# Three more column-pair groups of each up projection as 1024-column blocks with a seven-product pair, in a decoder trunk on one core

## The chip, the cores and the metric

The kernel runs on one core of a Trainium2 chip. The metric is the device time of one launch in microseconds, from the first instruction to the last of that core. The kernel before takes 2167.38 us as the median of three runs (2167.01 to 2168.72). A profile of one execution of it gives the rows quoted below.

## The reference

The input is x, 256 positions of 2048 features in float32. It passes one layer of gated linear attention, one layer of block attention (with 256 positions there is one block of keys, so it is plain causal attention with a position bias), and after each of them a gated ConvFFN. Each starts with an RMS norm and adds its result to x.

```
def conv_ffn(x, norm_w, w_up, conv_w, conv_b, w_down):
    S = x.shape[1]
    h = rms_norm(x, norm_w) @ w_up                 # 2048 -> 11264
    hp = jnp.pad(h, ((0, 0), (CONV_WIDTH - 1, 0), (0, 0)))
    acc = conv_b
    for j in range(CONV_WIDTH):
        acc = acc + conv_w[j] * hp[:, j:j + S]
    a, u = jnp.split(acc, 2, axis=-1)
    return (jax.nn.silu(a) * u) @ w_down           # 5632 -> 2048

h = h + gla_mixer(...)      # q, k, v, g = rms_norm(h) @ w_in; gated; @ w_out
h = h + conv_ffn(h, ...)
k, v = rms_norm(h) @ w_kv;  h = h + moba_mixer(h, ..., k, v)
h = h + conv_ffn(h, ...)
```

The two up projections (2048 x 11264) and the two down projections (5632 x 2048) are most of the work.

## The kernel before

**Matrix products.** TensorE works on operands that were split in two parts of reduced width: `whi` is the weight rounded by a cast on ScalarE (L151), `wlo` the rest, by a subtraction on VectorE (L153). The activations are kept the same way (`xw`: high half, then low half). A product is high x high + low x high + high x low, so three matmuls of 512 columns each. Two forms exist. `gemm_tok` (lines L305 and L308 in the profile) makes 512 output columns at a time: a step is one weight piece of 1024 columns (two rows of 128 features by 512 columns), 12 matmuls. `down` (L361) makes 1024 output columns and all 256 positions as a 2 x 2 grid of products per *pair* of 256 input features. A plain pair takes eight products in two steps of 12 matmuls, 24 in all. A pair marked + in `ORDERS` takes seven products (Strassen's scheme): 21 matmuls. For it VectorE makes sums of the weight (`t13`, `t24`: L112 to L114) that are split like weights, and sums of the activations: `whole` adds the high and low part of one pair (L328), `combine` makes four 128-wide parts from it (`comb`, L318 to L321), and splits them by a cast (L437, ScalarE) and a subtraction (L438, VectorE). At the end of a block VectorE adds the product sums up (`c`, L416 to L430).

**The weight stream.** Weights come by SP's queue in pieces of 128 x 2048 (`wraw`), and `WeightStream.prefetch` splits them a few steps ahead of TensorE, in rings of three buffers and more. `latest` holds the last pair of split instructions; what is issued under `behind()` is ordered after these two on its engine. Each engine runs its instructions in the order of its list, and that list is set by a scheduler before the launch, which can hoist instructions that depend on nothing late.

**Up projection.** Layer by layer, 22 column groups J of 512 columns (256 of the a half, 256 of the u half) run through `gemm_tok`. `square` scales the result (ScalarE) and transposes it (VectorE) into `z`; one step later POOL's queue stores it (`turned`), two steps later four POOL loads bring it back with features on the partitions (`upT`), and from step 7 `convolve` runs (ScalarE: `au`, then VectorE). `after(n, ...)` counts these steps of TensorE.

**Around it.** The gla gates (`gate`, `gated`) use the same way through memory, from step 12 for heads 2 and 3; their result `go` feeds the output projection. The k block, the g block and the mq block (1024 columns of k, g and the queries) use `down` with results that stay on chip (`DIRECT`). dn0 and dn1 are the down projections, with combinations that `convolve` makes early for pairs 1 to 13 (`EARLY`); pairs 15 and 17 go through `combine_parts`. At the start ACT's queue loads the norm weights `gn` and the first two pieces of x (`h`), while SP's queue loads the first weights in three cuts.

Of the kernel before, what the change touches and what calls it, by code (L numbers as in the profile page):

```python
# [37 lines left out]
def _order(text):  # L38

    words = text.replace("|", " ").split()  # L40
    return [(int(k.rstrip("+")), k.endswith("+")) for k in words], len(text.split("|")[1].split())
# [9 lines left out]
            _order("0 1+ 2 3+ 4 5+ 6 7+ 8 9+ 10 11+ 12 13+ 14 15+ 16 17+ 18+ | 19 20 21")],  # L51
    "k": [_order("0 1+ 2 3+ 4+ | 5 6 7")],
    "mq": [_order("0 1 2+ 3 4 | 5 6 7")],
    "g": [_order("0 2 5 1+ 3+ 4+ | 6 7")],
}
DIRECT = ("k", "mq", "g")


TURNS = ((0, (1, 2)), (0, (1, 2)), (1, (0, 1)), (1, (0, 1)), (1, (1, 2)), (1, (1, 2)))
# [108 lines left out]

@with_exitstack
def trunk(ctx: ExitStack, tc: tile.TileContext, xT, x_tok, cst, msk, w1p, w2a, w_k, w_qa, w_v2, w_v, w_gs, w_g, w_go,  # L170
          w_up0, w_dn0, w_kk, w_kv, w_mq, w_mqs, w_mo, w_up1, w_dn1, rel, onehot, out):
    nc = tc.nc
    V, A, T = nc.vector, nc.scalar, nc.tensor

# [1 line left out]
    big = ctx.enter_context(tc.tile_pool(name="big", bufs=38))  # L176
    raw = ctx.enter_context(tc.tile_pool(name="raw", bufs=3))
    parts = ctx.enter_context(tc.tile_pool(name="parts", bufs=3))
    tmp = ctx.enter_context(tc.tile_pool(name="tmp", bufs=6))
    small = ctx.enter_context(tc.tile_pool(name="small", bufs=2))  # L180
    banks = ctx.enter_context(tc.tile_pool(name="banks", bufs=8, space=PSUM))
    dram = ctx.enter_context(tc.tile_pool(name="dram", bufs=1, space=DRAM))
# [10 lines left out]
    def accs():  # L193
# [1 line left out]

    ws = WeightStream(tc, raw, parts)
    plan = [(w_v2, 1, 16384), (w_v, 2, 8192), (w_k, "k", None), (w_qa, 2, 8192), (w_gs, "g", None), (w_g, 2, 8192), (w_go, "go", None),
            (w_up0, FT // 2, 8192), (w_dn0, "dn0", None),
            (w_mq, (0,), 8192), (w_mqs, "mq", None), (w_mq, (1,), 8192), (w_kk, 4, 8192), (w_kv, 4, 8192), (w_mo, "mo", None),
            (w_up1, FT // 2, 8192), (w_dn1, "dn1", None)]  # L200
    for w, groups, cols in plan:
        if cols is None:
            for g, order in enumerate(ORDERS[groups]):
                ws.add_quads(w, g, order, groups in ("go", "mo"), groups == "mo")
            continue
        for g in range(groups) if isinstance(groups, int) else groups:
            ws.add(w, g, cols)
# [16 lines left out]
    V.memset(mhalf, -0.5)  # L224
    gn = keep.tile([128, KT], F32, name="gn")

    def load_x(p, queue=nc.sync):
        for i in range(2) if p == 0 else (slice(0, 2),):
            queue.dma_start(h[p][:, i], xT[p].rearrange("a (b c) -> a b c", b=2)[:, i])

    load_x(0, A)
    A.dma_start(gn, cst[:, C_GN:C_GN + KT])
    A.preload_act_table_set("natural_log_exp_and_others")
    load_x(1, A)

    ws.cuts = {0: ((0, 512), (512, 1024), (1024, 2048)), 1: ((0, 1024), (1024, 2048))}
    ws.lead[2, 0] = [lambda: nc.sync.dma_start(cs[:, :C_CW], cst[:, :C_CW])]
    for p, at in ((2, (1, 1024)), (3, (2, 0)), (4, (3, 0)), (5, (4, 0)), (6, (5, 0)), (7, (6, 0))):
        ws.lead.setdefault(at, []).append(lambda p=p: load_x(p))
# [44 lines left out]
    def after(steps, job):  # L284
        later.append((cur[0] + steps, job))
# [10 lines left out]
    def gemm_tok(xs, groups=1, evacuate=lambda ps: ps):  # L296
        out_ = [accs() for _ in range(groups)]
        for q0 in range(0, KT, 2):
            for ps in out_:
                hi, lo = step()  # L300
                for ks in ((0,), (1,)) if cur[0] < 3 and groups > 1 else ((0, 1),):
                    tiles_ = [(q0 + k, t, k * 512) for k in ks for t in range(2)]
                    for x0 in (0, S):
                        for kt, t, c in tiles_:
                            T.matmul(ps[t], xs(kt)[:, x0 + 128 * t:x0 + 128 * t + 128], hi[:, c:c + 512],  # L305
                                     start=kt == 0 and x0 == 0, stop=False)
                    for kt, t, c in tiles_:
                        T.matmul(ps[t], xs(kt)[:, 128 * t:128 * t + 128], lo[:, c:c + 512],  # L308
                                 start=False, stop=kt == KT - 1)
        got = out_ if groups > 1 else evacuate(out_[0])  # L310
        ws.prefetch(cur[0])
        return got
# [13 lines left out]
    def combine_parts(k, xs, into):  # L326
        t = temp("whole")
        V.tensor_add(t, xs[k][:, :, :S], xs[k][:, :, S:])  # L328
        combine(k, [(t[:, i, :128], t[:, i, 128:]) for i in range(2)], into)

    def sevens(name):
        return {k for order, _ in ORDERS[name] for k, seven in order if seven}

    def down(name, xs, combos, res, done, jobs):

        for b, (order, n_tail) in enumerate(ORDERS[name]):
            loaded = (name, b) != ("dn1", 1)
            new = [k for k, seven in order if seven and k not in combos]
            todo = {i: list(js) for i, js in jobs.get(b, {}).items()}
            for k in new:  # L340
                at = next(i for i, (k_, _) in enumerate(order) if k_ == k)
                todo.setdefault(max(at - 2, 0), []).append(lambda k=k: combine_parts(k, xs, combos))
            p = {}
            left = dict.fromkeys(range(1, 9), 0)
            for k, seven in order:
# [429 lines left out]
    down("g", nrm.xs, x_sums, None, gate_rows, {})  # L775
    for hd in (2, 3):
        z = gemm_tok(xs, 1, lambda ps: gate(hd, ps))
        through(hd, z, [(12 + i, lambda f, c=2 * hd + i: gated(c, f)) for i in range(2)])

    def ffn(layer, nrm, then):  # L780
        xs = rows(nrm.xs)
        hid, sums = [], {}
        whole = [None, None]
        cw = C_CW + layer * 3 * 2 * FT
        cb = C_CB + layer * 2 * FT
        turned = dram.tile([FT // 2, 16, 32, 4, 64], F32, name=f"turned{layer}")
# [12 lines left out]

        def load(J):  # L800
            f = slot([128, 4, S], F32, "upT")
            for q in range(4):
                nc.gpsimd.dma_start(f[32 * q:32 * q + 32].rearrange("p a (i c) -> p (a i) c", i=4),  # L803
                                  turned[J][:, :, q, :].rearrange("a r c -> r a c"))
            return f

        def convolve(j, t):
            au = temp("au")
            with ws.behind():
                for i in range(2):  # L810
                    n = i * FT + j
                    A.activation(au[:, i, :], t[:, i, :], AF.Identity, bias=col(cb + n),  # L812
                                 scale=col(cw + 2 * 2 * FT + n))
            for i in range(2):
                n = i * FT + j
                V.scalar_tensor_tensor(au[:, i, 1:], t[:, i, :S - 1], col(cw + 2 * FT + n), au[:, i, 1:],  # L816
                                       op0=OP.mult, op1=OP.add)
                V.scalar_tensor_tensor(au[:, i, 2:], t[:, i, :S - 2], col(cw + n), au[:, i, 2:],  # L818
                                       op0=OP.mult, op1=OP.add)
            A.activation(au[:, 0, :], au[:, 0, :], AF.Silu)  # L820
            V.tensor_mul(au[:, 0, :], au[:, 0, :], au[:, 1, :])
            if j % 2 == 0:
                hid.append(slot([128, 2, 2 * S], F32R, "hid"))
            split(hid[-1][:, j % 2, :S], hid[-1][:, j % 2, S:], au[:, 0, :])
            whole[j % 2] = (au[:, 0, :128], au[:, 0, 128:])
            if j % 2 and j // 2 in EARLY:
                combine(j // 2, whole, sums)

        f = {}
        for J in range(FT // 2):  # L830
            z = gemm_tok(xs, 1, square)
            after(1, lambda J=J, z=z: store(J, z))
            after(2, lambda J=J: f.update({J: load(J)}))
            for i in range(2):
                after(7 + 2 * i, lambda J=J, i=i: convolve(2 * J + i, f[J][:, 2 * i:2 * i + 2, :]))
        then(hid, sums)

    def scratch(name):
# [276 lines left out]

def _pairs(w):
    k, n = w.shape
    return _groups(w.reshape(k, 2, n // 256, 128).transpose(0, 2, 1, 3).reshape(k, n), 512)


def _buckets():
# [66 lines left out]
```

## Time and profile before

| | |
|---|---|
| time of the profiled execution | 2167.28 us |
| its span | 2165.5 us |
| start of the up projection of layer 0 | 375.56 us |
| start of dn0 | 855.2 us |
| mq block | 1108.6 us on |
| start of the up projection of layer 1 | 1454.54 us |
| start of dn1 | 1934 us |
| loads of `upT` | 176, 4.9 us from issue to landing (median) |

A page of the profile gives busy time by engine, the chain of work that ended last, and groups of instructions (line, engine, operation, count, busy time and mean length, idle time before them and what ended it). PE is TensorE's matmul row, PEld its weight loads, DVE is VectorE, ACT ScalarE, POOL GpSimd, SP the sync engine. Matmuls are pipelined: the length shown for one (0.39 us) is not the spacing between two starts. In a timeline, each row has the start, the length from the first start to the last end, and in brackets the idle time before it and what ended it.

### The profile page before, as it was taken

The numbers are of one execution on the slowest core, as the hardware profiler recorded it, in microseconds if no ns is written. First come the engines' busy times: TensorE is split into PE (matmuls) and PEld (weight loads), VectorE is DVE, ScalarE is ACT, GpSimd is POOL, SyncE is SP. The second block draws the span as 40 slices with busy tenths as digits, with TensorE's granted clock in tenths as the row PEclk, the third lists the DMA queues.
The fourth block names the chain that finished last, engine by engine and source line by source line (L and its number), as shares of the span: only waits on it lengthen the run. The fifth ranks groups of instructions, "written<-read, shape, count | busy, mean of one in ns | idle before, by whom it ended". The sixth has DMA issues, their size and how long they took to land.

```text
span 2165.5 us, 27041 instructions
## 1 busy us (share of the span) xinstructions
PE 2158.0 (100%) x9666; PEld 1789.5 (83%) x9666; DVE 1671.6 (77%) x2317; ACT 1301.1 (60%) x1881; POOL 291.5 (13%) x448
## 2 busy tenths in 40 slices
PE   9999999999999999999999999999999999999999
PEld 7888888888888888888888888888888888888887
DVE  6787788677777767898977787775777777779987
ACT  7656665565655656555566676565656565655554
POOL 1011111111111111000022241011111111110000
PEclk9999999999999999999999999999999999999999
DMA  8465676677777777675676887566787777775655
GB/s 321 178 232 196 214 263 241 219 234 251 236 247 237 247 237 244 212 253 211 234 262 246 269 270 240 213 234 225 236 248 235 249 235 248 237 252 214 233 199 171
DMA packets 90313, 510.10 MB, mean 236 GB/s; under 512 B 13714, under 2 KB 14754, under 8 KB 40259
## 3 DMA queue, kind: packets, MB, share of 16 engines
q1 hardware_dynamic: 60290, 417.05, 55.5%
q0 software_dynamic: 29024, 90.28, 14.6%
q8 instruction: 75, 1.23, 0.2%
q10 hardware_dynamic: 864, 1.06, 0.1%
q14 instruction: 60, 0.48, 0.1%
HBM read 463.22 MB, written 45.11 MB: 235 GB/s over the span
## 4 chain that ended last, share of the span: by engine, by line
PE 99%; DMA 1%; DVE 0%; ACT 0%; issue 0%; ACTq 0%; DVEq 0%
PE acc L305 42%; PE p L361 34%; PE acc L308 21%; PE hf L859 0%; DMA wraw<-w_go 0%; PE sT L705 0%; PE o L722 0%; PE s L972 0%; DMA h<-xT 0%; PE z L562 0%; PE o L508 0%; PE s L970 0%; DVE wlo L153 0%; PE o L507 0%; PE o L506 0%; PE o L505 0%
## 5 line engine op out<-in xcount | busy, mean ns | idle before, releaser
L153 DVE TENSOR_TENSOR wlo<-wraw,whi 128x1024 fp32r<-128x1024 f32 (+1 forms) x786 | 924.1, 1186 | 379.8 <-ACT whi L151 363.6
L151 ACT CAST whi<-wraw 128x1024 fp32r<-128x1024 f32 (+1 forms) x786 | 794.9, 1021 | 630.0 <-PE acc L305 390.6
L305 PE MATMUL acc<-whi,xw 128*128 128x512 f32 x3456 | 856.5, 390 | 1.3 <-ACT xw L268 1.3
L305 PEld LDWEIGHTS acc<-whi,xw 128*128 128x128 f32 x3456 | 648.9, 188 | 136.9 <-ACT xw L268 2.0
L308 PE MATMUL acc<-wlo,xw 128*128 128x512 f32 x1728 | 463.6, 390 | 0.0
L308 PEld LDWEIGHTS acc<-wlo,xw 128*128 128x128 f32 x1728 | 324.7, 188 | 67.4
L361 PE MATMUL p<-whi,hid 128*128 128x512 f32 x1058 | 284.4, 389 | 0.0
L361 PEld LDWEIGHTS p<-whi,hid 128*128 128x128 f32 x1058 | 198.4, 188 | 41.1
L151 ACT CAST whi<-t 128x1024 fp32r<-128x1024 f32 x100 | 102.9, 1052 | 84.6 <-PE p L361 70.4
L361 PE MATMUL p<-wlo,hid 128*128 128x512 f32 x529 | 153.1, 389 | 0.0
L803 POOL DMA_DIRECT2D upT<-turned x176 | 114.1, 655 | 147.1 <-DMA turned<-z 58.2
L153 DVE TENSOR_TENSOR wlo<-t,whi 128x1024 fp32r<-128x1024 f32 x100 | 119.9, 1221 | 15.0 <-PE p L361 8.1
L361 PE MATMUL p<-whi,comb 128*128 128x512 f32 x400 | 129.8, 389 | 0.0
L305 PE MATMUL acc<-whi,xkv 128*128 128x512 f32 x512 | 127.9, 391 | 0.0
L797 POOL DMA_DIRECT2D turned<-z x44 | 34.1, 775 | 679.1 <-DVE au L816 572.9
L361 PEld LDWEIGHTS p<-wlo,hid 128*128 128x128 f32 x529 | 99.3, 188 | 20.6
L305 PEld LDWEIGHTS acc<-whi,xkv 128*128 128x128 f32 x512 | 94.6, 188 | 18.7
L812 ACT ACTIVATE au<-upT,cs 128x256 f32<-128x256 f32 x176 | 95.8, 593 | 17.3 <-DMA upT<-turned 17.3
L361 PEld LDWEIGHTS p<-whi,comb 128*128 128x128 f32 x400 | 75.0, 188 | 15.5
L361 PE MATMUL p<-whi,xw 128*128 128x512 f32 x314 | 82.9, 389 | 0.0
L816 DVE SCALAR_TENSOR_TENSOR au<-upT,cs,au 128x255 f32<-128x255 f32 x176 | 77.0, 472 | 6.3 <-ACT au L812 6.1
L818 DVE SCALAR_TENSOR_TENSOR au<-upT,cs,au 128x254 f32<-128x254 f32 x176 | 80.5, 478 | 0.0
(241 smaller groups left out, 1897.5 us busy)
## 6 DMA issues: line engine op xcount, KB each, us to landing
wraw<-w_up SPq DMA_DIRECT2D x176, 1024.0 KB, 5.2
wraw<-w_dn SPq DMA_DIRECT2D x88, 1024.0 KB, 5.0
turned<-z POOLq DMA_DIRECT2D x44, 512.0 KB, 3.5
upT<-turned POOLq DMA_DIRECT2D x176, 128.0 KB, 4.9
wraw<-w_go SPq DMA_DIRECT2D x16, 1024.0 KB, 5.9
wraw<-w_kk SPq DMA_DIRECT2D x16, 1024.0 KB, 5.9
wraw<-w_kv SPq DMA_DIRECT2D x16, 1024.0 KB, 5.9
wraw<-w_mo SPq DMA_DIRECT2D x16, 1024.0 KB, 4.9
```

What stands on the lines that cost most here:

```text
L151: one = nc.scalar.copy(hi[:, a:b], src[:, a:b])
L153: two = nc.vector.tensor_sub(lo[:, a:b], src[:, a:b], hi[:, a:b].bitcast(F32))
L305: T.matmul(ps[t], xs(kt)[:, x0 + 128 * t:x0 + 128 * t + 128], hi[:, c:c + 512], start=kt == 0 and x0 == 0, stop=False)
L308: T.matmul(ps[t], xs(kt)[:, 128 * t:128 * t + 128], lo[:, c:c + 512], start=False, stop=kt == KT - 1)
L361: T.matmul(p[n], x[xi], w[wi][:, 512 * f:512 * f + 512], start=n not in begun, stop=left[n] == 0)
L797: nc.gpsimd.dma_start(turned[J].rearrange("(a i) r q c -> (i r) a (q c)", a=4), z.rearrange("p (a q) t c -> p a (q t c)", a=4))
L803: nc.gpsimd.dma_start(f[32 * q:32 * q + 32].rearrange("p a (i c) -> p (a i) c", i=4), turned[J][:, :, q, :].rearrange("a r c -> r a c"))
L812: A.activation(au[:, i, :], t[:, i, :], AF.Identity, bias=col(cb + n), scale=col(cw + 2 * 2 * FT + n))
L816: V.scalar_tensor_tensor(au[:, i, 1:], t[:, i, :S - 1], col(cw + 2 * FT + n), au[:, i, 1:], op0=OP.mult, op1=OP.add)
L818: V.scalar_tensor_tensor(au[:, i, 2:], t[:, i, :S - 2], col(cw + n), au[:, i, 2:], op0=OP.mult, op1=OP.add)
```

## The change

Four things are changed in the kernel. First, in each layer's up projection the groups J = 0, 4, 8 and 12 are each joined with the next one to a block of 1024 columns through `down("up", ..., only=b)`. Block 0 has two seven-product pairs, blocks 1 to 3 one. The other 14 groups stay in `gemm_tok`. The convolution starts at step 9, but for the last two groups. Second, `combine_parts` is issued under `behind()` in every `down`. Third, the gates' products of heads 2 and 3 start at steps 10 and 11, and the order of the first loads is set. Fourth, `temp` buffers go from 6 to 7, and the scratch of the software DMA from 4096 to 2048 bytes.

```diff
+    "up": [_order("0 1 2 3+ 4 5+ | 6 7")] + [_order("0 1 2 3+ 4 | 5 6 7")] * 3,
-DIRECT = ("k", "mq", "g")
+DIRECT = ("k", "mq", "g", "up")
+BLOCKS = (0, 4, 8, 12)
+GROUPS = [j for j in range(FT // 2) if j not in BLOCKS and j - 1 not in BLOCKS]
...
-    tmp = ctx.enter_context(tc.tile_pool(name="tmp", bufs=6))
+    tmp = ctx.enter_context(tc.tile_pool(name="tmp", bufs=7))
...
-    def load_x(p, queue=nc.sync):
-        for i in range(2) if p == 0 else (slice(0, 2),):
-            queue.dma_start(h[p][:, i], xT[p].rearrange("a (b c) -> a b c", b=2)[:, i])
-
-    load_x(0, A)
-    A.dma_start(gn, cst[:, C_GN:C_GN + KT])
-    A.preload_act_table_set("natural_log_exp_and_others")
-    load_x(1, A)
+    def load_x(p, i=slice(0, 2), queue=nc.sync):
+        return queue.dma_start(h[p][:, i], xT[p].rearrange("a (b c) -> a b c", b=2)[:, i])
+
+    begun = load_x(0, 0, A)
+    with tc.issue_after(begun.ins):
+        begun = A.dma_start(gn, cst[:, C_GN:C_GN + KT])
+    with tc.issue_after(begun.ins):
+        A.preload_act_table_set("natural_log_exp_and_others")
+        load_x(1, queue=A)
...
+    ws.lead[0, 0] = [lambda: load_x(0, 1)]
...
+    def combine_late(k, xs, into):
+        with ws.behind():
+            combine_parts(k, xs, into)
+
-    def down(name, xs, combos, res, done, jobs):
+    def down(name, xs, combos, res, done, jobs, only=None):
 
         for b, (order, n_tail) in enumerate(ORDERS[name]):
+            if only not in (None, b):
+                continue
...
-                todo.setdefault(max(at - 2, 0), []).append(lambda k=k: combine_parts(k, xs, combos))
+                todo.setdefault(max(at - 2, 0), []).append(lambda k=k: combine_late(k, xs, combos))
...
-        through(hd, z, [(12 + i, lambda f, c=2 * hd + i: gated(c, f)) for i in range(2)])
+        through(hd, z, [(8 + hd + i, lambda f, c=2 * hd + i: gated(c, f)) for i in range(2)])
...
-        f = {}
+        f, first = {}, {}
+
+        def onto(J, z):
+            after(1, lambda: store(J, z))
+            after(2, lambda: f.update({J: load(J)}))
+            for i in range(2):
+                after((9 if J < FT // 2 - 2 else 7) + 2 * i, lambda i=i: convolve(2 * J + i, f[J][:, 2 * i:2 * i + 2, :]))
+
+        def up_rows(t, J, x):
+            if t == 0:
+                first[J] = slot([128, 16, 2, 32], F32, "z")
+            A.activation(x, x, AF.Copy, scale=nrm.woven[:, t:t + 1])
+            V.transpose(first[J][:, :, t, :], x.rearrange("p (a b) -> p a b", b=32))
+            if t:
+                onto(J, first[J])
+
+        x_sums = {}
         for J in range(FT // 2):
-            z = gemm_tok(xs, 1, square)
-            after(1, lambda J=J, z=z: store(J, z))
-            after(2, lambda J=J: f.update({J: load(J)}))
-            for i in range(2):
-                after(7 + 2 * i, lambda J=J, i=i: convolve(2 * J + i, f[J][:, 2 * i:2 * i + 2, :]))
+            if J in BLOCKS:
+                b = BLOCKS.index(J)
+                down("up", nrm.xs, x_sums, None, lambda t, c, x: up_rows(t, J + c - 2 * b, x), {}, b)
+            elif J in GROUPS:
+                onto(J, gemm_tok(xs, 1, square))
...
-    nc = bacc.Bacc("TRN2", target_bir_lowering=False, num_devices=1, dynamic_dma_scratch_size=4096)
+    nc = bacc.Bacc("TRN2", target_bir_lowering=False, num_devices=1, dynamic_dma_scratch_size=2048)
```

The rest of the diff lays the weights out for it (`w_up0s`, `w_up1s` for the blocks, `w_up0`, `w_up1` for the groups that stay) and adds them to the plan of the stream.

What `behind()` does to the order shows in the k block. VectorE's rows there, from before the high part whi_1008 of the second seven-product pair is subtracted; `comb_1000` and `comb_1005` are the combination of the third pair, `t24_959` is the last weight sum of the second pair, `t13_1026` the first of the third. Before:

```order
L153 TENSOR_TENSOR wlo_974<-wraw_830,whi_973 128x1024
L112 TENSOR_TENSOR t13_1026<-wraw_891 128x1024
L438 TENSOR_TENSOR comb_1005<-comb_1000,comb_1005 128x4x128
L114 TENSOR_TENSOR t24_959<-wraw_857,t24_959 128x512
L153 TENSOR_TENSOR wlo_988<-wraw_857,whi_987 128x512
L153 TENSOR_TENSOR wlo_1009<-wraw_857,whi_1008 128x1024
L113 TENSOR_TENSOR t24_1027<-t13_1026,wraw_891 128x512
L153 TENSOR_TENSOR wlo_1032<-t13_958,whi_1031 128x1024
L153 TENSOR_TENSOR wlo_1048<-t24_959,whi_1047 128x1024
```

And now:

```order
L156 TENSOR_TENSOR wlo_988<-wraw_857,whi_987 128x512
L341 TENSOR_TENSOR whole_998<-xw_275 128x512
L117 TENSOR_TENSOR t24_959<-wraw_857,t24_959 128x512
L156 TENSOR_TENSOR wlo_1009<-wraw_857,whi_1008 128x1024
L156 TENSOR_TENSOR wlo_1032<-t13_958,whi_1031 128x1024
L331 TENSOR_TENSOR comb_1000<-whole_998 128x128
L333 TENSOR_TENSOR comb_1000<-whole_998 128x128
L332 TENSOR_TENSOR comb_1000<-comb_1000,whole_998 128x128
L334 TENSOR_TENSOR comb_1000<-whole_998,comb_1000 128x128
L115 TENSOR_TENSOR t13_1026<-wraw_891 128x1024
L457 TENSOR_TENSOR comb_1005<-comb_1000,comb_1005 128x4x128
L156 TENSOR_TENSOR wlo_1048<-t24_959,whi_1047 128x1024
```

The whole and the four parts of the third pair, which stood some fifty rows ahead, now stand among the weights of the second. ScalarE's rows at the same place, before:

```order
L437 CAST comb_1005<-comb_1000 128x4x128
L151 CAST whi_987<-wraw_857 128x512
L151 CAST whi_1008<-wraw_857 128x1024
L151 CAST whi_1031<-t13_958 128x1024
L151 CAST whi_1047<-t24_959 128x1024
L151 CAST whi_1054<-wraw_891 128x512
```

And now:

```order
L154 CAST whi_987<-wraw_857 128x512
L154 CAST whi_1008<-wraw_857 128x1024
L154 CAST whi_1031<-t13_958 128x1024
L456 CAST comb_1005<-comb_1000 128x4x128
L154 CAST whi_1047<-t24_959 128x1024
L154 CAST whi_1054<-wraw_891 128x512
```

The cast of the combination passed from ahead of the second pair's weights to a place in front of their last, whi_1047.

In the mq block (seven-product pair 2) VectorE has, before, with `whole_9251` and `comb_9253` of that pair:

```order
L328 TENSOR_TENSOR whole_9251<-xw_8189 128x512
L153 TENSOR_TENSOR wlo_9174<-wraw_9059,whi_9173 128x1024
L318 TENSOR_TENSOR comb_9253<-whole_9251 128x128
L320 TENSOR_TENSOR comb_9253<-whole_9251 128x128
L153 TENSOR_TENSOR wlo_9190<-wraw_9059,whi_9189 128x1024
L319 TENSOR_TENSOR comb_9253<-comb_9253,whole_9251 128x128
L153 TENSOR_TENSOR wlo_9213<-wraw_9124,whi_9212 128x1024
L112 TENSOR_TENSOR t13_9207<-wraw_9171 128x1024
L321 TENSOR_TENSOR comb_9253<-whole_9251,comb_9253 128x128
```

And now, behind the queries' scaling and transposes that follow the block of columns before (the same tiles have the numbers 9373 and 9375):

```order
L981 TENSOR_TENSOR q_9350<-q_9350,rr_9359 128x1024
L537 STREAM_TRANSPOSE z_9362<-q_9350 128x4x4x32 x2
L156 TENSOR_TENSOR wlo_9366<-wraw_9246,whi_9365 128x1024
L341 TENSOR_TENSOR whole_9373<-xw_8311 128x512
L156 TENSOR_TENSOR wlo_9401<-wraw_9293,whi_9400 128x512
L156 TENSOR_TENSOR wlo_9422<-wraw_9293,whi_9421 128x1024
L331 TENSOR_TENSOR comb_9375<-whole_9373 128x128
L333 TENSOR_TENSOR comb_9375<-whole_9373 128x128
L156 TENSOR_TENSOR wlo_9440<-t13_9329,whi_9439 128x1024
L332 TENSOR_TENSOR comb_9375<-comb_9375,whole_9373 128x128
L334 TENSOR_TENSOR comb_9375<-whole_9373,comb_9375 128x128
L457 TENSOR_TENSOR comb_9380<-comb_9375,comb_9380 128x4x128
```

The combination passed behind the queries' reduction, scaling and transposes and between the low parts of its own pair.

More of the change, by code (lines that the diff above doesn't have):

```diff
@@ L170, in trunk @@
 def trunk(ctx: ExitStack, tc: tile.TileContext, xT, x_tok, cst, msk, w1p, w2a, w_k, w_qa, w_v2, w_v, w_gs, w_g, w_go,
-          w_up0, w_dn0, w_kk, w_kv, w_mq, w_mqs, w_mo, w_up1, w_dn1, rel, onehot, out):
+          w_up0s, w_up0, w_dn0, w_kk, w_kv, w_mq, w_mqs, w_mo,
+          w_up1s, w_up1, w_dn1, rel, onehot, out):
     nc = tc.nc
@@ L197, in trunk @@
     plan = [(w_v2, 1, 16384), (w_v, 2, 8192), (w_k, "k", None), (w_qa, 2, 8192), (w_gs, "g", None), (w_g, 2, 8192), (w_go, "go", None),
-            (w_up0, FT // 2, 8192), (w_dn0, "dn0", None),
+            (w_up0s, w_up0, "up"), (w_dn0, "dn0", None),
             (w_mq, (0,), 8192), (w_mqs, "mq", None), (w_mq, (1,), 8192), (w_kk, 4, 8192), (w_kv, 4, 8192), (w_mo, "mo", None),
-            (w_up1, FT // 2, 8192), (w_dn1, "dn1", None)]
+            (w_up1s, w_up1, "up"), (w_dn1, "dn1", None)]
     for w, groups, cols in plan:
+        if cols == "up":
+            for J in range(FT // 2):
+                if J in BLOCKS:
+                    ws.add_quads(w, BLOCKS.index(J), ORDERS["up"][BLOCKS.index(J)], False, False)
+                elif J in GROUPS:
+                    ws.add(groups, GROUPS.index(J), 8192)
+            continue
         if cols is None:
@@ L329, in combine_parts @@
         combine(k, [(t[:, i, :128], t[:, i, 128:]) for i in range(2)], into)
+    def combine_late(k, xs, into):
+        with ws.behind():
+            combine_parts(k, xs, into)
     def sevens(name):
         return {k for order, _ in ORDERS[name] for k, seven in order if seven}
-    def down(name, xs, combos, res, done, jobs):
+    def down(name, xs, combos, res, done, jobs, only=None):
         for b, (order, n_tail) in enumerate(ORDERS[name]):
+            if only not in (None, b):
+                continue
             loaded = (name, b) != ("dn1", 1)
@@ L827, in convolve @@
                 combine(j // 2, whole, sums)
-        f = {}
-        for J in range(FT // 2):
-            z = gemm_tok(xs, 1, square)
-            after(1, lambda J=J, z=z: store(J, z))
-            after(2, lambda J=J: f.update({J: load(J)}))
-            for i in range(2):
-                after(7 + 2 * i, lambda J=J, i=i: convolve(2 * J + i, f[J][:, 2 * i:2 * i + 2, :]))
+        f, first = {}, {}
[12 more added lines that the diff above has]
+        x_sums = {}
+        for J in range(FT // 2):
+            if J in BLOCKS:
+                b = BLOCKS.index(J)
+                down("up", nrm.xs, x_sums, None, lambda t, c, x: up_rows(t, J + c - 2 * b, x), {}, b)
+            elif J in GROUPS:
+                onto(J, gemm_tok(xs, 1, square))
         then(hid, sums)
@@ L1117, in _pairs, with _columns @@
     k, n = w.shape
-    return _groups(w.reshape(k, 2, n // 256, 128).transpose(0, 2, 1, 3).reshape(k, n), 512)
+    return w.reshape(k, 2, n // 256, 128).transpose(0, 2, 1, 3).reshape(k, n)
+def _columns(w, starts, width):
+    import numpy as np
+    w = _pairs(w)
+    return np.concatenate([w[:, 512 * j:512 * j + width] for j in starts], axis=1)
 def _buckets():
@@ L1166 @@
         "w_go": _quads(a["gla_w_out"][0], ORDERS["go"]),
-        "w_up0": _pairs(a["ffn_w_up"][0]),
+        "w_up0s": _quads(_columns(a["ffn_w_up"][0], BLOCKS, 1024), ORDERS["up"]),
+        "w_up0": _groups(_columns(a["ffn_w_up"][0], GROUPS, 512), 512),
         "w_dn0": _quads(a["ffn_w_down"][0], ORDERS["dn0"]),
@@ L1173 @@
         "w_mo": _quads(a["moba_w_out"][0], ORDERS["mo"]),
-        "w_up1": _pairs(a["ffn_w_up"][1]),
+        "w_up1s": _quads(_columns(a["ffn_w_up"][1], BLOCKS, 1024), ORDERS["up"]),
+        "w_up1": _groups(_columns(a["ffn_w_up"][1], GROUPS, 512), 512),
         "w_dn1": _quads(a["ffn_w_down"][1], ORDERS["dn1"]),
```

## The prediction

> **What bounds the kernel now.** I read the page's first part and its chain first, to see which engine sets the end; then TensorE's waits, to see how much of its time is not work; then windows, to see how much room the other engines have in each stage.
>
> ```profile
> span 2165.5 us, 27041 instructions
> PE 2158.0 (100%) x9666; PEld 1789.5 (83%) x9666; DVE 1671.6 (77%) x2317; ACT 1301.1 (60%) x1881; POOL 291.5 (13%) x448
> PE 99%; DMA 1%; DVE 0%; ACT 0%; issue 0%; ACTq 0%; DVEq 0%
> ```
>
> The answer on TensorE's waits (us in total, times, longest) has three rows:
>
> ```profile
> PE junk L223 <- POOL idle L220: 1.3, 1, 1.3
> PE acc L305 <- ACT xw L268: 1.3, 1, 1.3
> PE p L361 <- DVE go L438: 0.9, 1, 0.9
> ```
>
> TensorE is on 99% of the chain and waits 3.5 us of 2165.5. So a matmul taken out is worth its spacing, and any wait that the change makes is paid in full. The windows (PE, PEld, DVE, ACT, POOL busy, with counts) show the room that is left:
>
> ```profile
> 100.00:120.00 20.00, 20.00 (x89) 16.55 (x89) 19.54 (x24) 14.66 (x18) 0.00 (x0) 1.00 0.58 211
> 380.00:860.00 480.00, 480.00 (x2124) 397.61 (x2123) 344.54 (x505) 282.59 (x401) 71.47 (x106) 1.00 0.75 239
> ```
>
> The first lies in the k block, the second in the up projection of layer 0. VectorE is busy 98% in the one and 72% in the other, and the granted clock is 1.00 in both.
>
> **Matmuls removed: -6.80 us.** The spacing of matmuls is read from the timeline (start, length): twelve of them fill one step.
>
> ```profile
> 102.78 1.98 PE L361 MATMUL p<-whi,xw 128*128 128x512 f32 x8
> 104.59 1.07 PE L361 MATMUL p<-wlo,xw 128*128 128x512 f32 x4
> 105.50 0.61 PE L361 MATMUL p<-whi,xw 128*128 128x512 f32 x2
> ```
>
> (105.50 - 102.78) / 12 = 0.2267 us. A seven-product pair takes 21 matmuls where two plain steps take 24. Block 0 of a layer has two such pairs, blocks 1 to 3 one each: 5 x 3 x 2 layers = 30 matmuls, 30 x 0.2267 = 6.80 us. [...] The trace has 227 ns through whole stages, so the trace's spacing is used.
>
> **VectorE in the new blocks: 0.** Groups of instructions (busy, mean ns):
>
> ```profile
> L153 DVE TENSOR_TENSOR wlo<-t,whi 128x1024 fp32r<-128x1024 f32 x100 | 119.9, 1221 | 15.0 <-PE p L361 8.1
> L113 DVE TENSOR_TENSOR t<-t,wraw 128x512 f32<-128x512 f32 x50 | 34.3, 687 | 0.4
> L430 DVE TENSOR_TENSOR c<-c,p 128x512 f32<-128x512 f32 x32 | 21.0, 684 | 12.7 <-PE p L361 9.1 <-DMA c<-rows 3.3
> L318 DVE TENSOR_TENSOR comb<-whole 128x128 f32<-128x128 f32 x9 | 2.5, 282 | 0.0
> ```
>
> Over the eight blocks the change adds 64 additions of product sums (x 0.684 = 43.8 us), 10 + 20 weight sums (10 x 1.221, as wide as the low part in the first row, + 20 x 0.687 = 25.9), 10 more low parts of 1024 and 10 of 512 columns (10 x 1.221 + 10 x 0.687, the latter as L113, = 19.1) and 4 combinations (a whole and a low half at 0.684 like the additions, four parts at 0.282: 4 x 2.5 = 10.0): 98.8 us, 12.4 a block. Two column pairs now hold 344.54 / 480 x 192 x 0.2267 = 31.2 us of VectorE work, so a block gets 43.6 us in 189 x 0.2267 = 42.8 us of TensorE. By lengths it is full; but a length overlaps the next one's start (two 1024-wide low parts, 1.22 us each, take 2.36 in the row at 121.42 below), so some 10% is free. What covers the rest is the lead of the low parts:
>
> ```profile
> 395.90 1.23 DVE L153 TENSOR_TENSOR wlo<-wraw,whi 128x1024 fp32r<-128x1024 f32 x1 [1.50 <-ACT whi L151]
> 402.78 1.07 PE L308 MATMUL acc<-wlo,xw 128*128 128x512 f32 x4
> ```
>
> The split that ends at 397.13 is used two steps on, at 402.78: a lead of 5.65 us, which plain pairs after each block win back. Following the program's order with these durations I find 1.4 us or more left at every weight of the blocks, so nothing is charged. Bounds: no gain is possible, since TensorE doesn't wait there now; the upper end is the slower rival's. ScalarE's 31 further instructions lie in an engine 59% busy in that window, and the transposes of the output only change their source.
>
> **The k block: +2.5 us.** Before, the sums (whole) and parts (comb) of its three seven-product pairs are made when VectorE has gaps, long ahead:
>
> ```profile
> 72.15 0.27 DVE L320 TENSOR_TENSOR comb<-whole 128x128 f32<-128x128 f32 x1
> 72.36 0.67 DVE L328 TENSOR_TENSOR whole<-xw 128x512 f32<-128x512 f32 x1
> 72.96 0.41 DVE L568 TENSOR_TENSOR zaug<-zt,rstd_h 16x256 f32<-16x256 f32 x1
> ...
> 100.76 1.82 DVE L153 TENSOR_TENSOR wlo<-wraw,whi 128x512 fp32r<-128x512 f32 x2
> ...
> 118.22 2.00 ACT L151 CAST whi<-t 128x1024 fp32r<-128x1024 f32 x2
> ...
> 121.42 2.36 DVE L153 TENSOR_TENSOR wlo<-t,whi 128x1024 fp32r<-128x1024 f32 x2
> ```
>
> The change binds them behind the latest weight split, so they move into the window that is 98% busy. Start to start, a whole takes 0.60 (72.36 to 72.96), a comb part 0.20 (or up to its length where the next needs its result), a 1024-wide operation 1.14. From 102.5, where the pair of low parts that began at 100.76 ends, the new order puts 17.0 us of VectorE work (seven 1024-wide operations, 8.0; ten 512-wide, three whole among them, 6.2; twelve parts, 2.8), the third pair's last part at its end: 119.5. Behind it on ScalarE stand that pair's comb cast (0.64 in the mq fence below) and then the t24 high part of the second pair, whi_1047 (1.0, by the row at 118.22): 121.15. TensorE comes to that weight 60 matmuls after 105.50, at 119.1: **2.05 us** of wait. VectorE then makes a t13, the comb's low half, a t24 and the weight's low half by 122.95, where TensorE wants it at 122.5: **0.45** more. Bounds: 0, if gaps that I count as used let it catch up; 4, if waits I don't see, each below a step of 2.72, put one more operation ahead.
>
> ScalarE's order is what makes this dear. [...]
>
> **The mq block: +2.05 us.** Its one combination also moves, from before the block's first weights to behind them:
>
> ```profile
> 1110.80 1.22 DVE L941 TENSOR_REDUCE ss<-hsq 128x8 f32<-128x1024 f32 x1
> 1111.72 0.64 ACT L437 CAST comb<-comb 128x512 fp32r<-128x512 f32 x1
> 1113.38 1.66 POOL L944 TENSOR_TENSOR rr<-ss,mhalf 128x8 f32<-128x8 f32 x1 [7.54 <-DVE ss L942]
> 1115.08 1.23 DVE L946 TENSOR_TENSOR q<-q,rr 128x1024 f32<-128x1024 f32 x1 [1.78 <-POOL rr L944]
> 1116.34 1.31 DVE L518 STREAM_TRANSPOSE z<-q 128x512 f32<-128x512 f32 x2
> 1116.78 1.98 PE L361 MATMUL p<-whi,xw 128*128 128x512 f32 x8
> ```
>
> In the new order the small sum that feeds rr follows the reduction at once (1112.0), rr ends at 1113.95, q and the transposes at 1116.5. Then come a low part (1.14), whole (0.6), low parts of 512 and 1024 columns (0.6, 1.14), two parts (0.4), a low part (1.14) and two parts (0.55): 1122.1; the cast follows until 1122.9. TensorE wants it 18 matmuls after 1116.78, at 1120.86: 2.05 us. Bounds 0 and 3, for the same reasons. The late combinations of the down projections and of the blocks leave 1 us or more by the same walk; they cost nothing, or their part of rival 2.
>
> **The rest: -1.5 us.** The wait on go, and the start:
>
> ```profile
> 315.86 1.07 PE L361 MATMUL p<-whi,go 128*128 128x512 f32 x4
> 317.83 1.20 PE L361 MATMUL p<-whi,go 128*128 128x512 f32 x4 [0.90 <-DVE go L438]
> ```
>
> ```profile
> 0.74 0.42 ACTq L232 DMA_DIRECT2D gn<-cst  x1
> 1.19 0.93 ACTq L229 DMA_DIRECT2D h<-xT  x2
> 4.48 0.62 ACT L151 CAST whi<-wraw 128x512 fp32r<-128x512 f32 x1 [1.04 <-DMA wraw<-w_v]
> 5.82 0.51 ACT L268 ACTIVATE xw<-h,gn 128x256 fp32r<-128x256 f32 x1 [0.72 <-DMA h<-xT]
> ```
>
> Four matmuls from 315.86 end their slots at 316.77, so the gap before 317.83 is 1.06 us; the gate's products move one or two steps (2.7 or 5.4 us) ahead, and it goes: -1.06 (0 at worst). The first half of h is issued 0.45 us earlier, and xw waits for it: -0.45. It can't be under -0.72, since the first weight half is cast until 5.10; it is +0.45 if gn, now issued 0.45 later, is what lands last. The second half of h passes to SP's queue between two weight cuts (some 0.42 of issue, as the gn row), inside the same bounds.
>
> The smaller scratch could delay the loads of convolution input, on which ScalarE already waits:
>
> ```profile
> L812 ACT ACTIVATE au<-upT,cs 128x256 f32<-128x256 f32 x176 | 95.8, 593 | 17.3 <-DMA upT<-turned 17.3
> 873.98 1.09 ACT L812 ACTIVATE au<-upT,cs 128x256 f32<-128x256 f32 x2 [2.05 <-DMA upT<-turned]
> ```
>
> Two steps more (5.4 us) before the convolution cover it for 20 of 22 pairs in a layer; the last two keep the old 7. These 17.3 us delayed no matmul, so I take 0, and +2 a layer as the upper end (a load as late again as in the last row).
>
> **Sum.** -6.80 + 2.5 + 2.05 - 1.06 - 0.45 = -3.76. The profiled run took 2167.28 (span 2165.5 and 1.78 around it), 0.1 under the median shown of 2167.38; so 2163.5.
>
> **Rivals.** (1) *The combinations hide*: VectorE's true gaps absorb both moves. For it: before, TensorE lives through a VectorE that is 98% busy without one wait. Against it: the walks above miss by 2 us at each place. Without 4.55 us: 2159.0. (2) *They cost more, or loads come late*: k at 4, mq at 3, half of the load delay: 2163.5 + 1.5 + 0.95 + 2 = 2168.0. (3) *Slower: VectorE becomes the bound inside the blocks.* Place: the eight new blocks, full by lengths. It decides when a block sets VectorE back by more than the 5.65 us lead; each microsecond beyond is paid eight times, and from 1.0 us beyond the kernel is slower. If a quarter of a block (10.7 us) goes to VectorE's waits on ScalarE and TensorE, it ends 43.6 - 4.3 + 10.7 - 42.8 = 7.2 us late: 8 x 1.55 = 12.4, 2175.9. For it: in the up projection it idles 28%, on whi above all. Against it: in the k window, as full, only 2% was lost. [...]
>
> **How the numbers follow.** A measurement of this kernel tells about 0.2% (4.3 us) from no change. Forecast 0.45 (a third of it beyond the 0.2%, since it lies so close: 0.15 faster, 0.30 same), (1) 0.22 faster, (2) 0.20 (0.17 same, 0.03 slower), (3) 0.10 slower, (4) 0.03 same: faster 0.37, same 0.50, slower 0.13. The range leaves out (3) and the edges of (1) and (2): 2158.6 to 2169.0.
>
> **What would show it.** Right: TensorE has 30 matmuls less; its waits list comb (ScalarE) or whi with 2 us each near 119 and 1119, and no go; none in the up projections. Wrong: rows of wlo or c in the up projections among the waits (rival 3), au with more than 20 us behind upT and whi late (rival 2), or no wait at all beside the start (rival 1).

## The result, and the profile after

The changed kernel takes 2179.59 us (median of six runs, 2173.88 to 2187.48) against 2167.45 before (2166.59 to 2168.72): a ratio of 1.0055, 95% interval 1.0038 to 1.0071. It is slower by 12 us, and its runs spread over 14 us where those of before spread over 2. In the runs further below a few executions are far longer than the rest, whatever the kernel (5642 and 3110 us are two); the medians count them, the ratios leave them out. The profiled execution of the changed kernel took 2180.33, span 2178.6. The page's first part, and TensorE's waits (us in total, times, longest):

```profile
span 2178.6 us, 27184 instructions
PE 2157.0 (99%) x9636; PEld 1783.5 (82%) x9636; DVE 1751.2 (80%) x2455; ACT 1320.6 (61%) x1913; POOL 291.5 (13%) x448
PE 8%; DVE 1%; DMA 1%; issue 1%; ACT 0%; POOL 0%; POOLq 0%; ACTq 0%; DVEq 0%
```

```profile
PE p L380 <- ACT whi L154: 5.6, 6, 1.6
PE acc L318 <- ACT whi L154: 4.3, 1, 4.3
PE p L380 <- ACT comb L456: 2.2, 1, 2.2
PE junk L234 <- POOL idle L231: 1.3, 1, 1.3
PE p L380 <- DVE wlo L156: 1.1, 3, 0.4
PE acc L318 <- ACT xw L281: 1.0, 1, 1.0
```

The 30 matmuls are gone (x9666 to x9636) and so is the wait on go, but TensorE now waits 15.5 us instead of 3.5, 13.1 of them for ScalarE: for whi, for xw at the start, and once for comb. (The chain of the page can be followed back only to a load of upT at 1952.62 here, so its 8% for PE is no sign that TensorE stopped being the bound.) Two of these waits cost more than they last. Windows just behind them (the same columns as before; the clock is the number after POOL):

```profile
1119.00:1123.40 4.40, 3.70 (x11) 2.89 (x12) 3.46 (x4) 4.37 (x6) 3.68 (x7) 0.73 1.02 371
1612.00:1616.00 4.00, 3.70 (x9) 2.94 (x10) 4.00 (x7) 3.48 (x7) 2.39 (x4) 0.57 0.33 98
1600.00:1604.00 4.00, 4.00 (x20) 3.30 (x19) 1.22 (x1) 0.02 (x1) 0.00 (x0) 1.00 0.99 227
```

In the last window, ahead of a wait, the clock is 1.00 and 20 matmuls start in 4 us. Behind the 2.2 us wait of the mq block and the 4.3 us wait at 1612 it is 0.73 and 0.57, with 9 to 11 matmuls. The record of the clock shows two stretches of 3.41 us at half speed ahead of the last matmul in this execution, 1.7 us lost in each.

Where the 13.1 us of span come from. The waits are counted here as the spacing of two matmul starts beyond 0.2267 us, some 0.16 us more than the idle time in a row:

| | us |
|---|---|
| 30 matmuls | -6.8 |
| go, start | -1.06, -0.3 |
| k block (1.79 + 0.37) | +2.2 |
| mq block | +2.4 |
| down projection of layer 1, late combinations (at 2027, 2144, 2152 to 2155) | +4.4 |
| up projection of layer 1 and the start of dn1 (1568, 1572, 1612, 1972) | +6.5 |
| half clock, twice | +3.4 |
| from the last matmul to the end (4.0 to 5.9) | +1.9 |
| sum | 12.6 |

The row on layer 1's up projection has nothing to do with VectorE. The timeline up to the wait at 1612, behind layer 1's second block:

```profile
1588.98 0.77 POOL L816 DMA_DIRECT2D turned<-z  x1 [26.78 <-DVE z L860]
...
1595.62 1.95 POOL L822 DMA_DIRECT2D upT<-turned  x3 [5.86 <-DMA turned<-z]
...
1604.26 0.65 POOL L822 DMA_DIRECT2D upT<-turned  x1 [6.68 <-issue]
...
1610.22 1.09 ACT L831 ACTIVATE au<-upT,cs 128x256 f32<-128x256 f32 x2 [10.20 <-DMA upT<-turned]
...
1611.22 1.03 ACT L154 CAST whi<-wraw 128x1024 fp32r<-128x1024 f32 x1
...
1612.30 3.57 PE L318 MATMUL acc<-whi,xw 128*128 128x512 f32 x8 [4.30 <-ACT whi L154]
```

Of the four loads of a group, three are issued in a row, and the fourth 6.68 us after them, with nothing that POOL waited for ("issue"). ScalarE's au stands 10.20 us on that load; the weight cast behind it comes at 1611.22, and TensorE has waited 4.30 us for it. The trace's times of landing say what ends POOL's stand: the first of the three loads lands at 1603.95, 8.33 us after its issue, and the fourth goes out 0.31 us after that. It does so, 0.31 us after the first has landed, in all 44 groups of this trace. Groups of the same operations, of before and of the changed kernel, and of the changed kernel ScalarE's wait:

```profile
L803 POOL DMA_DIRECT2D upT<-turned x176 | 114.1, 655 | 147.1 <-DMA turned<-z 58.2 <-PE acc L305 55.1 <-issue 26.6
```

```profile
L822 POOL DMA_DIRECT2D upT<-turned x176 | 114.8, 657 | 329.9 <-issue 165.3 <-DMA turned<-z 53.5 <-ACT au L831 28.4
L831 ACT ACTIVATE au<-upT,cs 128x256 f32<-128x256 f32 x176 | 95.6, 594 | 54.1 <-DMA upT<-turned 54.1
```

The time that POOL's loads stand on nothing visible went from 26.6 to 165.3 us, and ScalarE's wait for loads from 17.3 to 54.1.

### The profile page after: what moved, and what is told of

It is laid out like the page before. It is cut to its first block, busy times and chain, and to the rows that moved or that the text cites. A ratio compares the mean times of both kernels' runs of the same rounds, so it can differ in the third digit from the quotient of the medians.

```text
span 2178.6 us, 27184 instructions
## 1 busy us (share of the span) xinstructions
PE 2157.0 (99%) x9636; PEld 1783.5 (82%) x9636; DVE 1751.2 (80%) x2455; ACT 1320.6 (61%) x1913; POOL 291.5 (13%) x448
## 5 line engine op out<-in xcount | busy, mean ns | idle before, releaser
L318 PE MATMUL acc<-whi,xw 128*128 128x512 f32 x2432 | 605.2, 390 | 5.3 <-ACT whi L154 4.3
L318 PEld LDWEIGHTS acc<-whi,xw 128*128 128x128 f32 x2432 | 456.4, 188 | 101.4 <-ACT whi L154 5.2
L321 PE MATMUL acc<-wlo,xw 128*128 128x512 f32 x1216 | 325.4, 389 | 0.0
L380 PE MATMUL p<-whi,xw 128*128 128x512 f32 x1238 | 319.6, 390 | 0.8 <-ACT whi L154 0.8
L380 PEld LDWEIGHTS p<-whi,xw 128*128 128x128 f32 x1238 | 232.5, 188 | 50.0 <-ACT whi L154 1.9
L321 PEld LDWEIGHTS acc<-wlo,xw 128*128 128x128 f32 x1216 | 228.5, 188 | 48.2 <-issue 0.6
L380 PE MATMUL p<-wlo,xw 128*128 128x512 f32 x619 | 172.1, 390 | 0.0
L156 DVE TENSOR_TENSOR wlo<-t,whi 128x1024 fp32r<-128x1024 f32 x120 | 144.5, 1220 | 25.4 <-ACT whi L154 20.8
L380 PE MATMUL p<-whi,comb 128*128 128x512 f32 x480 | 157.4, 393 | 7.0 <-ACT whi L154 4.7
L822 POOL DMA_DIRECT2D upT<-turned x176 | 114.8, 657 | 329.9 <-issue 165.3
L380 PEld LDWEIGHTS p<-wlo,xw 128*128 128x128 f32 x619 | 116.2, 188 | 24.3 <-DVE wlo L156 0.3
L831 ACT ACTIVATE au<-upT,cs 128x256 f32<-128x256 f32 x176 | 95.6, 594 | 54.1 <-DMA upT<-turned 54.1
```

The source lines that it names most:

```text
L156: two = nc.vector.tensor_sub(lo[:, a:b], src[:, a:b], hi[:, a:b].bitcast(F32))
L380: T.matmul(p[n], x[xi], w[wi][:, 512 * f:512 * f + 512], start=n not in begun, stop=left[n] == 0)
```

## The experiments

Two theories share the loss. RING: the scratch of 2048 bytes holds back the fourth load. LATE: the late combinations put ScalarE's weight casts behind them. Against both stands BLOCK, that VectorE can't keep up inside the new blocks. Times are medians; the kernels of one group ran on one chip, with the kernel before beside them.

**Scratch back at 4096**

```diff
-    tmp = ctx.enter_context(tc.tile_pool(name="tmp", bufs=7))
+    tmp = ctx.enter_context(tc.tile_pool(name="tmp", bufs=6))
-    nc = bacc.Bacc("TRN2", target_bir_lowering=False, num_devices=1, dynamic_dma_scratch_size=2048)
+    nc = bacc.Bacc("TRN2", target_bir_lowering=False, num_devices=1, dynamic_dma_scratch_size=4096)
```

> The changed kernel with the scratch of the software DMA back at 4096 bytes and, to make room for it, six temp buffers. Theory RING (the small scratch holds back the fourth upT load of a group, ScalarE stands on it and the weight casts queue behind): the waits of 0.45, 0.71 and 4.46 us near 1568 to 1612, the slow clock after the last (1.7) and 0.84 near 1972 go, 2179.6 - 8.2 = 2171.4 us, and the runs lie within 2 us of each other. Theory LATE (the late combinations cost nearly all): 2178 to 2181, au still waits some 50 us for upT. Theory TEMP (six temp buffers are too few for the blocks): above 2181.

Measured 2173.04 us (2170.65 to 2179.53), ratio 1.0018 (1.0000 to 1.0036). RING holds: the waits near 1568, 1612 and 1972 are gone, no fourth load is held back, and ScalarE waits 6.2 us for loads instead of 54.1:

```profile
L831 ACT ACTIVATE au<-upT,cs 128x256 f32<-128x256 f32 x176 | 95.2, 594 | 6.3 <-DMA upT<-turned 6.2
```

The waits in k, mq and dn1 stand as they were, one stretch of half clock with them. TEMP falls. The spread of 2 us that RING asked for did not come: it is 8.9. The edit changes the temp buffers too; that the scratch alone does it is shown by the kernel before with the small scratch, further below, which keeps six.

**Combinations as before**

```diff
-                todo.setdefault(max(at - 2, 0), []).append(lambda k=k: combine_late(k, xs, combos))
+                todo.setdefault(max(at - 2, 0), []).append(lambda k=k: combine_parts(k, xs, combos))
```

> The changed kernel with combine_parts as before, not under behind(). Theory LATE: the waits near 119 (2.2 with the low half), 1119 (2.4, and 1.7 of slow clock behind it) and in dn1 near 2027 and 2142 to 2155 (4.4) go: 2179.6 - 10.7 = 2168.9 us. Theory RING alone: 2178 to 2181. In both, the runs still spread by 5 us or more, since the small scratch stays.

Measured 2170.36 us (2164.1 to 2181.16, but for one execution of 5642; 2168.47 without it), ratio 1.0003 (0.9980 to 1.0026). TensorE's waits in this kernel's profile:

```profile
PE acc L318 <- ACT whi L154: 4.6, 2, 3.9
PE junk L234 <- POOL idle L231: 1.3, 1, 1.3
PE acc L318 <- ACT xw L281: 1.3, 1, 1.3
```

No comb, no waits in k, mq and dn1: LATE holds. What is left are two waits behind late loads in layer 1, and a spread of 17 us.

**Both edits**

> Both of the two edits before together: scratch 4096, six temp buffers, combine_parts as before. If RING and LATE are all that goes wrong, 2167.45 - 6.80 (30 matmuls) - 1.06 (go) - 0.3 (start) = 2159.3 us, TensorE waits below 4 us. Theory BLOCK (VectorE can't keep up inside the new blocks): above 2163, with waits on wlo or whi in the up projections.

Measured 2158.95 us (2157.48 to 2160.34), ratio 0.9950 (0.9935 to 0.9965). The page and the waits of this kernel:

```profile
PE 2151.8 (100%) x9636; PEld 1784.5 (83%) x9636; DVE 1749.6 (81%) x2455; ACT 1324.4 (61%) x1913; POOL 292.6 (14%) x448
...
PE 99%; DVE 0%; DMA 0%; issue 0%; ACT 0%; ACTq 0%; DVEq 0%
```

```profile
PE junk L234 <- POOL idle L231: 1.3, 1, 1.3
PE acc L318 <- ACT xw L281: 0.9, 1, 0.9
PE p L380 <- DVE wlo L156: 0.5, 1, 0.5
```

The eight blocks run without a wait of TensorE, with the same VectorE work in them. BLOCK falls, the two theories together explain the loss, and this version beats both kernels, by 0.5% against the one before. Its spread is 3 us.

**The kernel before, with the scratch at 2048**

```diff
-    nc = bacc.Bacc("TRN2", target_bir_lowering=False, num_devices=1, dynamic_dma_scratch_size=4096)
+    nc = bacc.Bacc("TRN2", target_bir_lowering=False, num_devices=1, dynamic_dma_scratch_size=2048)
```

> The kernel before with the scratch at 2048 bytes, nothing else. RING: with the convolution at step 7 the fourth upT load is late for most groups, au waits for upT rise from 17 us to over 50, and the kernel gets slower by 4 us or more with a wider spread. If the ring matters only beside the blocks: 2167.4, within 1.

Measured 2195.66 us (2170.36 to 2216.94), ratio 1.0096 (1.0063 to 1.0129), beside 2168.29 of the kernel before on that chip. This is RING with nothing else changed, and larger than expected: 21 us by the ratio, 27 by the medians. The profile's rows:

```profile
PE acc L305 <- ACT whi L151: 24.7, 17, 2.9
```

```profile
L803 POOL DMA_DIRECT2D upT<-turned x176 | 114.7, 656 | 273.8 <-issue 138.5 <-DMA turned<-z 60.3 <-PE acc L305 35.4
L812 ACT ACTIVATE au<-upT,cs 128x256 f32<-128x256 f32 x176 | 95.9, 594 | 174.3 <-DMA upT<-turned 174.3
```

**The same, with the convolution at step 9**

```diff
-                after(7 + 2 * i, lambda J=J, i=i: convolve(2 * J + i, f[J][:, 2 * i:2 * i + 2, :]))
+                after((9 if J < FT // 2 - 2 else 7) + 2 * i, lambda J=J, i=i: convolve(2 * J + i, f[J][:, 2 * i:2 * i + 2, :]))
```

> The kernel before with the scratch at 2048 and the convolution at step 9 (7 for the last two groups), no blocks. COVER (two more steps hide the late fourth load for plain groups, which come every 22 us; what is left in the changed kernel comes from the two groups of a block, stored within a few us of each other): 2167 to 2169, no waits on whi in the up projections, though au still waits. If the small ring delays loads by more than 5.4 us: above 2172, waits on whi in most groups.

Measured 2169.18 us (2166.44 to 2173.22, but for one execution of 3109.69), beside 2169.32 of the kernel before; ratio 0.9999 (0.9989 to 1.0009). COVER holds, and the rows show that POOL stands as long as in the run before:

```profile
L803 POOL DMA_DIRECT2D upT<-turned x176 | 114.6, 656 | 262.7 <-issue 140.5 <-DMA turned<-z 48.7 <-ACT au L812 40.8
L812 ACT ACTIVATE au<-upT,cs 128x256 f32<-128x256 f32 x176 | 95.8, 594 | 7.3 <-DMA upT<-turned 7.3
```

140.5 us of issue against 138.5, but ScalarE waits 7.3 us instead of 174.3: two steps are enough for plain groups. In the changed kernel they are not enough, because the fourth load goes out when the first has landed, and that takes longer beside the blocks: up to 8.3 us there and 9.4 in the run with early combinations, against 6.0 in this run. In the wait at 1612 the fourth load lands 14.5 us after the first was issued, and it belongs to the first group of its block. Why landing takes longer beside the blocks was not settled; it does so with 4096 bytes too (up to 9.3 us in the run with both edits, 5.9 in the kernel before). Beside it, the two groups of a block are stored shortly after each other, and the second store stands behind the first group's loads in POOL's queue. In the timeline of the run with both edits:

```profile
1579.49 0.77 POOL L816 DMA_DIRECT2D turned<-z  x1 [30.51 <-DVE z L860]
1586.17 2.59 POOL L822 DMA_DIRECT2D upT<-turned  x4 [5.91 <-DMA turned<-z]
1588.75 0.78 POOL L816 DMA_DIRECT2D turned<-z  x1
...
1596.76 2.60 POOL L822 DMA_DIRECT2D upT<-turned  x4 [7.23 <-DMA turned<-z]
```

With 4096 bytes all four loads go out together (the four in 2.59 and 2.60 us above), and step 9 is enough: au waits 13.2 us for loads in that run, and whi is not among TensorE's waits.

**Both edits, the convolution of every group at step 7**

> The run with both edits (2159.0), with the convolution of every group back at step 7; scratch 4096. If step 9 only makes up for the small scratch: 2159 to 2160. If the blocks themselves need it (two groups' loads close together): above 2162, with waits on whi behind au beside the blocks.

Measured 2231.59 us (2228.84 to 2248.31, four runs), ratio 1.0306 (1.0261 to 1.0352). The blocks themselves need step 9, and by far more than was expected:

```profile
PE p L380 <- ACT whi L154: 36.1, 11, 7.4
PE acc L318 <- ACT whi L154: 10.1, 6, 3.4
```

ScalarE's au waits 121.5 us for loads, 39 times. The waits make half clock in 10 stretches. No fourth load is held back here. In the wait that ends at 1608.54 (6.4 us) the four loads land up to 10.65 us after their issue, au stands 4.64 us on them, and the rest of the convolution and the cast of a combination then keep ScalarE until 1607.44, ahead of the weight casts. Why the loads land so late was not settled.

**Both edits, scratch 3072**

> The run with both edits, with a scratch of 3072 bytes in place of 4096. With 2048 the trace shows a store and three loads of a group go out and the fourth load wait. RING as a threshold (what counts is that the fourth load fits): 2159 to 2160, runs within 3 us. RING in proportion to the size: 2163 or more and a spread of 5 us.

Measured 2159.73 us, 2157.57 to 2166.72: of ten runs six lie between 2157.6 and 2160.2, four between 2165.9 and 2166.8. The profiled one is of the upper group and has one wait of 4.27 us behind au in layer 1 with half clock behind it. The threshold reading holds for the ring: in none of the 44 groups of this trace is the fourth load held back. The wait is of another kind, the second group of a block behind the first in POOL's queue:

```profile
1760.26 2.60 POOL L822 DMA_DIRECT2D upT<-turned  x4 [7.17 <-DMA turned<-z]
1762.85 0.78 POOL L816 DMA_DIRECT2D turned<-z  x1
...
1775.85 2.60 POOL L822 DMA_DIRECT2D upT<-turned  x4 [12.22 <-ACT whi L154]
...
1784.36 1.09 ACT L831 ACTIVATE au<-upT,cs 128x256 f32<-128x256 f32 x2 [5.33 <-DMA upT<-turned]
```

The second store takes 12.4 us to land, and the loads behind it go out 0.65 us after that; au stands 5.33 us on them. The wait and its half clock cost this execution 6.9 us without the ring, and runs within 3 us, as the threshold reading asked for, did not come. The kernel before spread from 2164.95 to 2184.38 on that chip.

**Late combinations in one place at a time** (from the run with both edits; the condition is the edit)

```diff
+(combine_late if name in ("k", "mq") else combine_parts)(k, xs, combos)
```

> Scratch 4096, six temp buffers, and the late combinations in the k and mq blocks alone. PLACE: 2.2 us of wait in k, 2.3 in mq and 1.7 us of slow clock behind the longer one, 2159.0 + 6.2 = 2165.2 us. If TensorE's loss is won back later, 2159 to 2161; if dn1 had taken most of it, below 2162.

Measured 2165.82 us (2162.26 to 2174.81), 2170.27 for the kernel before on that chip. The waits are those of the changed kernel: 1.8 and 0.4 us in k, 2.2 in mq, 4.4 together. The half clock did not follow in the profiled execution, and its span is 2161.3.

```diff
+(combine_late if name in ("dn0", "dn1") else combine_parts)(k, xs, combos)
```

> Scratch 4096, six temp buffers, and the late combinations in the two down projections alone (pairs 15 and 17). PLACE: the waits of dn1 seen in the changed kernel (1.2 near 2027, 1.3 near 2142, 2.0 near 2152), and a tail that is 1.5 to 2 us longer because the last additions and the accumulating loads start later: 2159 + 6 = 2165 us. If these waits came from the small scratch, 2159.

Measured 2165.64 us (2165.16 to 2172.62), 2169.32 before on that chip. The waits of dn1 and the longer tail are there with the large scratch: LATE has them. The timeline near 2014 in this kernel:

```profile
2010.73 1.22 DVE L156 TENSOR_TENSOR wlo<-t,whi 128x1024 fp32r<-128x1024 f32 x1 [0.59 <-PE p L380]
2011.87 0.68 DVE L341 TENSOR_TENSOR whole<-hid 128x512 f32<-128x512 f32 x1
...
2013.64 0.62 ACT L456 CAST comb<-comb 128x512 fp32r<-128x512 f32 x1 [3.52 <-DVE comb L334]
2014.17 1.04 ACT L154 CAST whi<-t 128x1024 fp32r<-128x1024 f32 x1
...
2015.26 0.50 PE L380 MATMUL p<-whi,comb 128*128 128x512 f32 x1 [1.01 <-ACT whi L154]
```

ScalarE stands 3.52 us on a combination that isn't wanted yet, and the high part that TensorE wants stands behind it.

```diff
+(combine_late if name == "up" else combine_parts)(k, xs, combos)
```

> Scratch 4096, six temp buffers, and the late combinations in the up projections' blocks alone. Theory PLACE (a late combination costs only where VectorE is full and the pair's weights wait behind it on ScalarE: k, mq, dn1): no cost here, 2159.0, within 1.5. Theory BIND (binding a combination behind the latest split costs wherever it stands): five combinations a layer, above 2163, with waits on comb or whi in the up projections.

Measured 2160.65 us (2157.94 to 2167.4), waits as in the run with both edits, but for one of 0.34 us in the output projection at 298.5 in place of the 0.5 in dn1. The median lies 0.15 us outside the 1.5 that PLACE allowed, far from BIND's 2163: inside the blocks a late combination costs nothing that can be told.

**The kernel before, with the new start and gates only**

> The kernel before with only the new order of the first loads and the earlier gates of heads 2 and 3: no blocks, scratch 4096. The wait on go (1.06 us) is gone and the first matmul starts 0.3 to 0.4 us earlier: 1.4 us under the kernel before, about 2166 to 2167 where that shows 2167.5 to 2168.3. [...]

Measured 2167.12 us (2164.2 to 2176.78) beside 2170.27; ratio 0.9974 (0.9951 to 0.9997). The wait on go is gone. The first matmul starts 0.15 us earlier than before (6.23 against 6.38), and waits 1.40 us for xw. Two waits on whi of 0.6 us each, behind au in layer 0, are new: ScalarE waits 70.4 us for loads in this execution, with a scratch of 4096 and no fourth load held back, so a long wait of au is by itself no sign of the ring. The distance to the run with both edits, by the lowest times, is 2164.2 - 2157.5 = 6.7 us, the price of 30 matmuls at 0.2267; they ran on different chips, but the lowest times of the two kernels with blocks that ran on this one, 2157.57 and 2157.94, give 6.6 and 6.3.

## Why the prediction was wrong

It forecast 2163.5 and a range to 2169.0; 2179.6 lies outside, on the slower side.

- *Matmuls, -6.80; go, -1.06; start, -0.45.* Right, but for the start, which brought 0.1 to 0.4 us in the profiles. With what spoils them taken away the kernel takes 2158.95, where these terms (the start at 0.3) gave 2159.3 in the expectation. The fourth chance, 0.03, is that of a matmul spacing shorter than 0.2267 us: no run shows one (0.2267 us is the median over twelve matmuls in a row in the traces of before and after alike), and the lowest times put the 30 matmuls at 6.3 to 6.7 us.
- *VectorE in the new blocks, 0.* Right; the slower rival, VectorE as the bound inside them, did not occur.
- *k, +2.5.* Right in place and kind: 2.2 us by the gaps, its end at 119.28, with the same weight waiting on ScalarE behind the cast of the third pair's combination.
- *mq, +2.05.* The wait was right, 2.4 us by the rows; mis-sized by what follows it, 1.7 us of half clock in this execution. The sum had no term for the clock at all.
- *"The late combinations of the down projections and of the blocks leave 1 us or more by the same walk."* This step failed for dn1. They cost 4.4 us of waits and 1.9 of tail in the profile, and the run with them alone is 2165.64. The prediction names the walk for dn1 but doesn't show it, so which of its steps went astray can't be read off. What the trace shows is that a low part ahead of the combination waits for TensorE (0.59 in the row at 2010.73), that ScalarE stands 3.52 us on the combination, and that the weight behind it comes 1.01 us late. For the blocks the step was right.
- *"These 17.3 us delayed no matmul, so I take 0, and +2 a layer as the upper end"*. This is the step that failed by most. The value was taken from a kernel in which a load was 2 us late; in the changed one the fourth load is held back for up to 6.7 us, and au stands up to 10.2. Waits and half clock of 8.2 us followed in the profile, twice the upper end of 4. Undoing it alone gained 8 us by the ratios to the kernel before (1.0055 and 1.0018), and 11.4 by the medians with the combinations early (2170.36 to 2158.95; 9.5 without the execution of 5642). The two steps of cover, 5.4 us, held for plain groups, as the run with the convolution at step 9 shows; beside the blocks the first load itself landed later (up to 8.3 us after its issue, against 6.0), for which the prediction had no term.
- These terms, 8.2 us for the loads, 6.3 for dn1 and 1.7 for the clock behind mq, make 16.2 of the 16.8 us by which the profiled execution (2180.33) lies above the forecast.
- The spread of 14 us was not foreseen, and its cause is not shown. The kernel before spreads over 33 us with the small scratch and step 7, its two longest executions left out, but over 7 with it and step 9, and over 19 with the large one on one chip.

The second rival (combinations that cost more, loads that come late) was the right kind, at 2168.0 where it should have had 2180.

## What to carry to other kernels

A change of buffer space that pays for another one (here two kilobytes of DMA scratch for one more temp buffer) is the first thing to undo when a kernel gets slower. An operation that is bound late because nothing needs it earlier still has others listed behind it on its engine (here ScalarE stood 3.52 us on a combination, and TensorE then 1.01 us on the weight cast behind it): look at what stands behind it, not at who reads it. A wait of two microseconds on a TensorE that else hardly idles (3.5 us of 2165.5 here) should be priced with the 1.7 us of half clock that followed the 2.2 us wait in the mq block.

## What the runs showed of the hardware

With a scratch of 2048 bytes POOL issues three loads of 128 KB behind a 512 KB store and then stands for 1.0 to 7.7 us. In all 44 groups of each of the four traces with 2048 bytes, the fourth load goes out 0.31 us after the first has landed; with 3072 and 4096 bytes no fourth load is held back, and all go out some 0.65 us apart. What POOL stands on in that time is in no record.

Half clock followed some short waits of TensorE and not others, and the traces tell which. Within a trace all stretches of half clock begin on one grid of 3.413 us: the two of the changed kernel begin at 1121.05 and 1612.57, 144 such windows apart. They last one window or several (3.41, 6.83, and once 10.24 us in the run with step 7). In some 8200 windows at full clock of all thirteen traces, half clock followed each of the 17 in which TensorE's rows leave 2.0 us or more idle, and none of those with 1.64 or less; of three in between, 1.78 and 1.79 drew it and 1.94 did not. So in these traces it matters where a wait falls on the grid:

| wait | us | idle in its windows | half clock behind it |
|---|---|---|---|
| mq, scratch back at 4096 | 2.03 | 2.03 | 3.41 |
| mq, late combinations in k and mq | 2.03 | 0.77, 1.26 | none |
| layer 1, combinations as before | 3.89 | 2.12, 1.77 | 6.83 |
| layer 1, changed kernel | 4.30 | 1.16, 3.14 | 3.41 |

(In the second row the grid is taken from the half clock behind the last matmul.) The grid lies 0.8 to 3.1 us off the span's start in the six executions that have such a stretch ahead of their last matmul, 1.48 us in the changed kernel.
